# A hybrid transformer layer: attention values for four heads in one pass, the compressed branch laid among two delta-rule projections, and five staging tiles

## The chip, the core and the metric

The kernel runs on one core of a Trainium2 chip. A core has TensorE (PE in the rows; its weight loads are PEld), VectorE (DVE), ScalarE (ACT), GpSimd (POOL), and the queue of SyncE (SP), from which all transfers between HBM and the core's memory (SBUF) are issued here, in order. Matmul results land in banks of PSUM, from which VectorE and ScalarE copy them out. The metric is the time of one execution in microseconds; lower is better.

## The reference, cut to what matters

One layer works on 1024 tokens of width 1024, in fp32. Its input projection feeds three attention branches of 8 heads in 2 groups, and a gated delta rule of 4 heads; a feed-forward part follows.

```python
h = rmsnorm(x, norm1_g)
proj = h @ w_in
nsa_q, nsa_kv, nsa_gate, gdn_qkv, gdn_z, gdn_b, gdn_a = jnp.split(proj, SPLIT_POINTS, axis=-1)
...
o_cmp, p_cmp = nsa_compressed(q, k_cmp, kv[:, :, 1], cmp_pos, cmp_w1, cmp_w2)
idx = nsa_select_indices(p_cmp, T)
o_slc = nsa_selected(q, k_slc, kv[:, :, 3], idx)
o_win = nsa_window(q, k_win, kv[:, :, 5])
o_nsa = gates[..., 0:1] * o_cmp + gates[..., 1:2] * o_slc + gates[..., 2:3] * o_win
o_gdn = gdn_mixer(gdn_qkv, gdn_z, gdn_b, gdn_a, gdn_conv_w, gdn_a_log, gdn_dt_bias, gdn_norm_g)
x = x + jnp.concatenate([o_nsa, o_gdn], axis=-1) @ w_out
h = rmsnorm(x, norm2_g)
x = x + (jax.nn.silu(h @ w_gate) * (h @ w_up)) @ w_down
```

The compressed branch gathers overlapping blocks of 32 tokens' keys and values, adds a learned position to each token, sends each block through a small two-layer network (`cmp_w1`, a tanh form of the activation, `cmp_w2`), and attends to the 63 resulting vectors.

## The kernel before

A product of full precision is made of three matmuls: each operand is split into a rounded high half and a low half (ScalarE copies the high half, VectorE or GpSimd subtracts to get the low one), and `split3` (lines 119 to 121) issues high x high, high x low and low x high. The order of the work on each engine is not written by hand: an instruction scheduler places the rows, and the tile pools (tag and number of buffers) limit it.

*Start, 0 to 90 us.* x is staged in `xraw` tiles (3 buffers), split into `xh` and `xl`, and `proj_tok(c)` multiplies it, eight units of 128 tokens each, by pieces 0, 1 and 2 of the token-major weights. `wprep` loads weights in pieces through `wraw` (DMA L203), splits them on ScalarE (L205) and GpSimd (L208). `evac_z` stores what pieces 0 and 1 give, through `zt` tiles, to `zD`. Between them, x by tokens (`xN`) is loaded into the same `xraw` tiles and squared on ScalarE (L266), which gives `rstd1`, and the angles of the rotary embedding are worked out on VectorE and ScalarE (up to the sine, L307). Piece 2 is the compressed branch's keys and values; `evac_cmp` scales a unit into a `ck` tile (L331) and rotates it on GpSimd (L317 to L322).

*Compressed branch, 90 to 108 us.* `cmp_blocks` transposes the eight `ck` tiles (L340) into banks `b`; copies on VectorE (L345) and ScalarE (L346) lay them out by block into `kdt`; VectorE adds the positions (L360); 2 x 32 fp32 matmuls with `w1t` follow (L365), then tanh (L369), `hy` (L370) and the products with `w2t` (L375, L384), which end in `kch`, `kcl` and `vcs`. Zero tiles `zz` are stored to `uD` and `tD` (L398). Then the PSUM pool `psa` is closed and `pps` opened.

*Delta rule, 108 to 466 us.* `gdn_proj(ft)` (48 matmuls of 512 columns, a convolution, a store to `gD`) for ft = 0, 4, 1, 5, 2, 6, 3, 7, then the rest of the delta rule.

*Attention, 466 to 785 us.* 16 units (128 tokens, one group of 4 heads). `prep_q` loads `qt`, `scores` makes the window probabilities `Pw`, the selected ones `Ps` (two heads to a tile) and the compressed ones `PC`, `values` multiplies them with values. `merge` interleaves the scores of the next unit, the values of this one and a filler (`wob`: the delta rule's half of the output projection) by the costs that each yields or declares (`wa`, `wc`). `values(u)` goes over the unit's blocks once for each pair of heads `hp`: two blocks' transposes (4 of 128x128) fill a bank `b`, ScalarE (L1067) and VectorE (L1068) split it into `PT`, and, three `PT` tiles later, products of 256 columns (L1045) add into one bank `c`. After each pass ScalarE copies half of `c` to `otmp` (L1049) and VectorE adds the other half into `mn` (L1050).

*Feed-forward, from 785 us.* Not touched.

## Time and profile before

| | |
|---|---|
| median of 3 runs | 1499.25 us (1497.87 to 1504.8) |
| profiled execution | 1494.86 us, span 1493.1 us |
| TensorE | busy 1426.7 us, 96% of the span |
| its weight loads | 1220.1 us, 82% |
| VectorE | 966.9 us, 65% |
| ScalarE | 723.5 us, 48% |
| GpSimd | 708.1 us, 47% |
| mean granted clock | 0.985 of full speed |

The span runs from the first to the last instruction of the profiled execution. Matmuls overlap each other in the rows, so a duration of a matmul is longer than the distance to the next start; where matmuls follow each other, starts are compared. Shares are means over stages with different limits.

### The profile page before, as it was taken

Reading aid. Unit: us, or ns where it says so; the run is one execution under the profiler, and the core shown is the slowest. Engines: PE = TensorE matmul, PEld = TensorE weight load, DVE = VectorE, ACT = ScalarE, POOL = GpSimd, SP = SyncE. Lnnn points to the kernel's source line nnn. Section 1 sums busy time; section 2 is a strip of 40 time slices with the busy share of each in tenths; the row PEclk is TensorE's granted clock in tenths of the full one; section 3 lists DMA queues with packets and bytes.
Section 4 is the critical chain, followed back from the end, with each engine's and each line's share of the span. In section 5 each row is a group of like instructions: output and inputs, shape, how many; then the busy total and the mean of one; then the engine's idle time right before and its main releaser. Section 6 shows DMA issues by size and latency. Waiting matters only on the chain.

```text
span 1493.1 us, 23452 instructions
## 1 busy us (share of the span) xinstructions
PE 1426.7 (96%) x7984; PEld 1220.1 (82%) x7984; DVE 966.9 (65%) x2286; ACT 723.5 (48%) x1604; POOL 708.1 (47%) x755
## 2 busy tenths in 40 slices
...
GB/s 250 300 68 78 92 171 162 126 194 208 203 119 202 101 54 107 47 22 44 36 123 244 36 87 99 83 78 85 78 86 85 85 92 274 200 119 134 1 0 113
DMA packets 142743, 174.96 MB, mean 117 GB/s; under 512 B 26912, under 2 KB 79392, under 8 KB 142496
## 3 DMA queue, kind: packets, MB, share of 16 engines
...
q8 instruction: 63, 1.03, 0.3%
q14 instruction: 56, 0.46, 0.1%
...
## 4 chain that ended last, share of the span: by engine, by line
PE 60%; DVE 10%; issue 5%; ACT 5%; POOL 4%; DMA 2%; SPq 0%; POOLq 0%; ACTq 0%; DVEq 0%
PE mm L119 16%; PE mm L121 16%; PE mm L120 16%; PE c L1045 3%; PE b L1065 2%; DVE PT L1068 2%; ACT Ps L1016 1%; PE a L637 1%; DVE cy L429 1%; PE a L999 1%; PE a L644 1%; ACT PT L1067 1%; DMA wraw<-in_w_out 1%; POOL w L208 1%; DMA mgt<-mgD 1%
## 5 line engine op out<-in xcount | busy, mean ns | idle before, releaser
L1202 POOL TENSOR_TENSOR A<-wq,A 128x512 fp32r<-128x512 f32 x94 | 126.4, 1346 | 97.8 <-ACT A L1201 76.5
L1201 ACT ACTIVATE A<-wq 128x512 fp32r<-128x512 f32 x96 | 60.1, 630 | 135.0 <-PE mm L121 118.3
L119 PE MATMUL mm<-w,xh 128*128 128x256 f32 x384 | 112.2, 292 | 6.3 <-ACT w L205 3.9
L1068 DVE TENSOR_TENSOR PT<-b,PT 128x512 fp32r<-128x512 f32 (+2 forms) x168 | 103.8, 621 | 18.8 <-ACT PT L1067 17.0
L120 PE MATMUL mm<-w,xh 128*128 128x256 f32 x384 | 112.0, 292 | 1.0 <-POOL w L208 1.0
L121 PE MATMUL mm<-w,xl 128*128 128x256 f32 x384 | 111.9, 291 | 0.0
L1202 POOL TENSOR_TENSOR wk<-wq,wk 128x512 fp32r<-128x512 f32 x61 | 82.6, 1355 | 53.0 <-ACT wk L1201 44.7
L1067 ACT ACTIVATE PT<-b 128x512 fp32r<-128x512 f32 (+2 forms) x168 | 89.0, 538 | 37.4 <-PE b L1065 33.2
L1045 PE MATMUL c<-PT,vs 128*128 128x256 f32 x528 | 92.9, 300 | 0.1
L208 POOL TENSOR_TENSOR w<-wraw,w 128x512 fp32r<-128x512 f32 x48 | 63.5, 1337 | 60.6 <-ACT w L205 34.6
L1201 ACT ACTIVATE wk<-wq 128x512 fp32r<-128x512 f32 x63 | 39.6, 630 | 85.4 <-PE mm L121 78.5
L119 PEld LDWEIGHTS mm<-w,xh 128*128 128x128 f32 x384 | 75.3, 196 | 6.9 <-ACT w L205 4.1
L119 PE MATMUL mm<-T,A 128*128 128x512 f32 x200 | 79.2, 396 | 0.0
L120 PE MATMUL mm<-T,A 128*128 128x512 f32 x200 | 79.2, 396 | 0.0
L121 PE MATMUL mm<-T,A 128*128 128x512 f32 x200 | 79.2, 396 | 0.0
L1479 POOL TENSOR_TENSOR ring<-ring,ring 128x512 f32<-128x512 f32 x44 | 58.2, 1324 | 40.1 <-DVE ring L1464 26.5
L120 PEld LDWEIGHTS mm<-w,xh 128*128 128x128 f32 x384 | 75.5, 196 | 1.3 <-POOL w L208 1.2
L119 PE MATMUL mm<-xh,w 128*128 128x512 f32 x192 | 75.7, 394 | 0.0
L121 PEld LDWEIGHTS mm<-w,xl 128*128 128x128 f32 x384 | 75.4, 196 | 0.1
L121 PE MATMUL mm<-xh,w 128*128 128x512 f32 x192 | 75.3, 392 | 0.0
L1045 PEld LDWEIGHTS c<-PT,vs 128*128 128x128 f32 x528 | 73.0, 192 | 2.5 <-DVE PT L1068 0.3
L120 PE MATMUL mm<-xl,w 128*128 128x512 f32 x192 | 74.9, 390 | 0.0
...
## 6 DMA issues: line engine op xcount, KB each, us to landing
...
```

The lines of the kernel that those rows point to most:

```text
L119: after(mm(ps, lhsT=lh, rhs=rh, start=first, stop=False, skip_group_check=grow), prev)
L120: mm(ps, lhsT=lh, rhs=rl, start=False, stop=False, skip_group_check=grow)
L121: return mm(ps, lhsT=ll, rhs=rh, start=False, stop=last, skip_group_check=grow)
L208: (lo or G).tensor_tensor(out=wt[:, 1, k0:k0 + n, :], in0=raw, in1=f32(wt[:, 0, k0:k0 + n, :]), op=ALU.subtract)
L429: V.scalar_tensor_tensor(out=y, in0=cr[:, j:j + 512], scalar=cw[:, j:j + 1], in1=y, op0=ALU.mult, op1=ALU.add)
L1045: mm(po[:, 0:256], lhsT=v, rhs=PT[0:K, a, b_ * 256:(b_ + 1) * 256], start=(n_ == 0 and a == 0), stop=(last and b_ == len(vs) - 1 and a == 1))
L1065: tpose(pt[:, o_:o_ + P], src[:, hh, b * P:(b + 1) * P], ident)
L1067: act(out=PT[0:K, 0, 0:w], in_=pt[0:K, 0:w], func=AF.Copy)
L1068: V.tensor_tensor(out=PT[0:K, 1, 0:w], in0=pt[0:K, 0:w], in1=f32(PT[0:K, 0, 0:w]), op=ALU.subtract)
L1201: act(out=dst[:, 0], in_=src, func=AF.Copy)
L1202: after(eng.tensor_tensor(out=dst[:, 1], in0=src, in1=f32(dst[:, 0]), op=ALU.subtract), prev)
L1479: G.tensor_tensor(out=t, in0=half[o], in1=t, op=ALU.mult)
```

## The change

1. *Staging.* `xraw` has 5 buffers; the raw pieces of the first weights have a tag of their own, `w0raw`; the first x tile is loaded in two halves with the weights between; `wprep` stages through 4 raw tiles (the output projections keep 3). Small tiles (`lowr`, `sm`, `cs16`, `sn16`, `kch`, `kcl`) lie in another pool.
2. *Compressed branch.* `cmp_blocks(i - 1)` is called from `evac_cmp(i)`; the position adds come in pieces of 128x256 for each half of the tokens, those of jj = 0 on VectorE, those of jj = 1 on GpSimd. `w1t`, `w2t` and `cpt` are loaded ahead of `proj_tok(2)`. `gdn_proj` takes the bank function as an argument; `gdn_proj(0)` stands ahead of the 64 matmuls with `w1t`, `gdn_proj(4)` between them and the tanh.
3. *Values.* One pass over the blocks for all four heads: four transposes (one block, four heads), one split, two products of 512 columns; `otmp` and `mn` once for each unit. `Ps` has 4 buffers, `qt` 1; `wx` of the filler comes from the pool `pmx`, whose 3 buffers it shares with the mean's squares.

```diff
-    def wprep(src, K, w, lo=None, tag="w", bufs=2, pl=None, rawbufs=3, rawpl=None, hi=None):
+    def wprep(src, K, w, lo=None, tag="w", bufs=2, pl=None, rawbufs=4, rawpl=None, hi=None):
...
+    XB = 5
     for k in range(KD):
-        r = mk(p1, [P, T], "xraw", F32, 3)
-        dma(r, xT[:, k, :])
-        raw = mk(pw, [P, TOKW[0]], "wraw", F32, 3)
-        dma(raw, tok_src(0)[:, k, :])
+        r = mk(p1, [P, T], "xraw", F32, XB)
+        raw = mk(p1, [P, TOKW[0]], "w0raw", F32, XB)
+        for hf in range(2 if k == 0 else 1):
+            xs = slice(hf * 512, (hf + 1) * 512) if k == 0 else slice(0, T)
+            dma(r[:, xs], xT[:, k, xs])
+            if hf == 0:
+                dma(raw, tok_src(0)[:, k, :])
...
-        r = mk(p1, [P, D], "xraw", F32, 3)
+        r = mk(p1, [P, D], "xraw", F32, XB)
         dma(r, xN[i * P:(i + 1) * P, :])
...
+        if i > 0:
+            cmp_blocks(i - 1)
...
+                for jj in range(2):
+                    pos_j = cpt[:, a, 8 * jj:8 * jj + 8].unsqueeze(2)
+                    for g in range(2):
+                        (V if jj == 0 else G).tensor_tensor(out=kdt[a][jj][:, :, g, n0:n0 + 32],
+                                                            in0=kdt[a][1][:, :, g, n0:n0 + 32],
+                                                            in1=bc(pos_j, [P, 8, 32]), op=ALU.add)
...
-    proj_tok(2, evac_cmp, banka)
-    for i in range(NT):
-        cmp_blocks(i)
     w1t = mk(p1, [P, 2, 16, P], "w1t")
     dma(w1t, cw1)
...
+    proj_tok(2, evac_cmp, banka)
+    cmp_blocks(NT - 1)
+    gdn_proj(0, banka)
...
     for a in range(2):
...
-        for j in range(2):
-            pos_j = cpt[:, a, 8 * j:8 * j + 8].unsqueeze(2)
-            V.tensor_tensor(out=kdt[a][j].rearrange("p r g n -> p r (g n)"),
-                            in0=kdt[a][1].rearrange("p r g n -> p r (g n)"), in1=bc(pos_j, [P, 8, P]), op=ALU.add)
-        psh = banka("mm")
+        psh = pshs[a] = banka("mm")
...
+    gdn_proj(4, banka)
+    for a in range(2):
+        psh = pshs[a]
...
     for h in range(4):
-        gdn_proj(h)
-        gdn_proj(4 + h)
+        if h:
+            gdn_proj(h, bank)
+            gdn_proj(4 + h, bank)
...
-        qt = mk(pk, [P, 256], "qt", F32, 2)
+        qt = mk(pk, [P, 256], "qt", F32, 1)
...
-                Ps[hp] = mk(pn, [P, 2, T], "Ps", F32, 3)
+                Ps[hp] = mk(pn, [P, 2, T], "Ps", F32, 4)
...
+        Pw, Ps = u["Pw"], u["Ps"]
+        blocks = [None] + [(Pw, b, VS[:, i - np_ + b, 2 + g, :]) for b in range(np_ + 1)]
+        blocks += [(Ps, b, VS[:, b, g, :]) for b in range(i + 1)]
+        po = bank("c")
+
+        def products(n_, K, v, PT):
+            for a in range(2):
+                mm(po, lhsT=v, rhs=PT[0:K, a], start=(n_ == 0 and a == 0), stop=(n_ == len(blocks) - 1 and a == 1))
...
+        for n_, blk in enumerate(blocks):
+            pt = bank("b")
+            for h in range(4):
...
+            PT = mk(pn, [P, 2, 512], "PT", F32R, LAG + 1)
+            act(out=PT[0:K, 0], in_=pt[0:K], func=AF.Copy)
+            V.tensor_tensor(out=PT[0:K, 1], in0=pt[0:K], in1=f32(PT[0:K, 0]), op=ALU.subtract)
+            todo.append((n_, K, v, PT))
+            if len(todo) > LAG:
+                products(*todo.pop(0))
+            yield 0.6
...
+        tmp = mk(pn, [64, 512], "otmp", F32, 1)
+        act(out=tmp, in_=po[64:128], func=AF.Copy)
         for hp in range(2):
...
+            V.tensor_tensor(out=mn[hp * 64:(hp + 1) * 64, g * 2:g * 2 + 2, i * P:(i + 1) * P],
+                            in0=po[0:64, hp * 256:(hp + 1) * 256].rearrange("p (h t) -> p h t", h=2),
+                            in1=tmp[:, hp * 256:(hp + 1) * 256].rearrange("p (h t) -> p h t", h=2), op=ALU.add)
...
-        wx = mk(pn, [P, 512], "wx", F32, WXB)
+        wx = flat(mk(pmx, [P, 4, P], "wx", F32, 3))
...
-        return [0.3 + 0.35 + n * 0.3] * 2
+        return [0.6 * (n + 1) + 0.9]
```

**First place: TensorE behind the last projection.** Before, the last transposes (L340, from `ck` tiles into banks `b`) stand directly ahead of the matmuls with `w1t` (L365), and the first delta projection (`w_1136`) behind all of them.

```order
L340 MATMUL b_1038<-cst_75,ck_977 128x128
L340 MATMUL b_1038<-cst_75,ck_1010 128x128
L365 MATMUL mm_1062<-kdt_101_733,w1t_1054 128x126 [waits DMAHW7_49,DVE_49]
L365 MATMUL mm_1062<-kdt_101_733,w1t_1054 128x126 x7
L365 MATMUL mm_1062<-kdt_102_734,w1t_1054 128x126 [waits DVE_49,Activation_49]
L365 MATMUL mm_1062<-kdt_102_734,w1t_1054 128x126 x7
L375 MATMUL mm_1085<-hy_1079,w2t_1056 128x126 [waits DMAHW4_49,DVE_49]
```

Now (lines 373 and 401 are those transposes and matmuls, `w_1077` the weights of `gdn_proj(0)`, `w_1194` those of `gdn_proj(4)`; the left-out rows between are more of the same projection):

```order
L373 MATMUL b_985<-cst_75,ck_1014 128x128 [waits Activation_49,Pool_49]
L373 MATMUL b_987<-cst_75,ck_1014 128x128
L119 MATMUL mm_1086<-xh_89,w_1077 128x512
L120 MATMUL mm_1086<-xl_90,w_1077 128x512
L373 MATMUL b_987<-cst_75,ck_1049 128x128 [waits Activation_49]
L121 MATMUL mm_1086<-xh_89,w_1077 128x512
L373 MATMUL b_985<-cst_75,ck_1049 128x128 [waits Pool_49]
...
L121 MATMUL mm_1123<-xh_89,w_1077 128x512
L401 MATMUL mm_1160<-kdt_101_734,w1t_738 128x126 [waits DMAHW4_49,DVE_49]
L401 MATMUL mm_1160<-kdt_101_734,w1t_738 128x126 x7
L401 MATMUL mm_1160<-kdt_102_735,w1t_738 128x126 [waits Pool_49]
L401 MATMUL mm_1160<-kdt_102_735,w1t_738 128x126 x7
```

All 48 matmuls of `gdn_proj(0)` now stand between the last transposes and the first matmul with `w1t`.

**Second place: SP's queue ahead of proj_tok(2).** Before, three of its four weight pieces (`wraw` from `in_w_tok`) are issued ahead of `w1t`, and the fourth behind the store of `zt_604`, the sixth tile of `proj_tok(1)`:

```order
L203 DMA wraw_738<-in_w_tok 128x512 [waits DMAHW2_49,Pool_49]
L253 DMA zD_58<-zt_520 128x256 [waits DMAHW3_49,Activation_49]
L203 DMA wraw_742<-in_w_tok 128x512 [waits DMAHW4_49,Pool_49]
L203 DMA wraw_746<-in_w_tok 128x512 [waits DMAHW5_49,Pool_49]
L253 DMA zD_58<-zt_548 128x256 [waits DMAHW6_49,Activation_49]
L352 DMA w1t_1054<-in_cw 128x4096 [waits DMAHW7_49,PE_49]
L253 DMA zD_58<-zt_576 128x256 [waits DMAHW0_49,Activation_49]
L253 DMA zD_58<-zt_604 128x256 [waits DMAHW1_49,Activation_49]
L203 DMA wraw_750<-in_w_tok 128x512 [waits DMAHW2_49,Pool_49]
```

Now (`zt_605` is that sixth tile):

```order
L388 DMA w1t_738<-in_cw 128x4096 [waits DMAHW4_49,PE_49]
L257 DMA zD_58<-zt_549 128x256 [waits DMAHW5_49,Activation_49]
L257 DMA zD_58<-zt_577 128x256 [waits DMAHW6_49,Activation_49]
L390 DMA w2t_740<-in_cw 128x192 [waits DMAHW7_49]
L257 DMA zD_58<-zt_605 128x256 [waits DMAHW0_49,Activation_49]
L392 DMA cpt_742<-in_cpos 128x32 [waits DMAHW1_49]
L203 DMA wraw_745<-in_w_tok 128x512 [waits DMAHW2_49,Pool_49]
L203 DMA wraw_749<-in_w_tok 128x512 [waits DMAHW3_49,Pool_49]
L257 DMA zD_58<-zt_633 128x256 [waits DMAHW4_49,Activation_49]
L203 DMA wraw_753<-in_w_tok 128x512 [waits DMAHW5_49,Pool_49]
L203 DMA wraw_757<-in_w_tok 128x512 [waits DMAHW6_49,Pool_49]
```

All four pieces moved behind `w1t` and the sixth tile's store, the last two behind the seventh's too.

**Third place: TensorE in a unit's values.** Before, at the change from one pass to the next, the new pass opens bank `c` again and waits for VectorE:

```order
L1065 MATMUL b_6368<-cst_75,Ps_6153 128x128 [waits DVE_49,PE_49]
L1065 MATMUL b_6368<-cst_75,Ps_6153 128x128 x3
L999 MATMUL a_6380<-kss_788_4406,QS_5976 128x512 [waits PE_49]
L1045 MATMUL c_6376<-PT_6302,vcs_91 128x256 [waits DVE_49]
L1045 MATMUL c_6376<-PT_6302,vcs_91 128x256
L999 MATMUL a_6380<-kss_789_4407,QS_5976 128x512
L1045 MATMUL c_6376<-PT_6317,vs_5143 128x256 x4
```

Now a unit opens `c` once, with products of 512 columns (transposes L1062, products L1051):

```order
L1062 MATMUL b_6419<-cst_75,Pw_6140 128x128 x2
L1062 MATMUL b_6419<-cst_75,Pw_6201 128x128 x2
L1051 MATMUL c_6358<-PT_6364,vcs_85 128x512 [waits Activation_49]
L1051 MATMUL c_6358<-PT_6364,vcs_85 128x512
L1062 MATMUL b_6429<-cst_75,Pw_6140 128x128 [waits DVE_49]
L1062 MATMUL b_6429<-cst_75,Pw_6140 128x128
L1062 MATMUL b_6429<-cst_75,Pw_6201 128x128 x2
L1051 MATMUL c_6358<-PT_6383,vs_5156 128x512 [waits Activation_49]
```

Each bank `b` takes one block of two `Pw` (or `Ps`) tiles, four heads, and two wide products follow it where two to four narrow ones stood.

## Rows read from the trace of the kernel before

**Rows 1.** The page: the span, TensorE's busy time, and from the table of costliest groups the two halves of the PT split, all forms together (line, engine, operation, out<-in shapes, count | busy us, mean ns | idle time before and its releaser).

```profile
span 1493.1 us, 23452 instructions
...
PE 1426.7 (96%) x7984; PEld 1220.1 (82%) x7984; DVE 966.9 (65%) x2286; ACT 723.5 (48%) x1604; POOL 708.1 (47%) x755
...
L1068 DVE TENSOR_TENSOR PT<-b,PT 128x512 fp32r<-128x512 f32 (+2 forms) x168 | 103.8, 621 | 18.8 <-ACT PT L1067 17.0
...
L1067 ACT ACTIVATE PT<-b 128x512 fp32r<-128x512 f32 (+2 forms) x168 | 89.0, 538 | 37.4 <-PE b L1065 33.2
```
**Rows 2.** Busy time by stretch of the span, in the projection and compressed stage (stretch, its length, busy us and instructions of PE, PEld, DVE, ACT, POOL, then the mean granted clock, the DMA share and GB/s).

```profile
57.60:70.00 12.40, 7.52 (x51) 7.12 (x51) 6.96 (x34) 5.03 (x12) 4.03 (x7) 0.84 0.85 319
...
90.40:96.00 5.60, 2.09 (x18) 1.64 (x16) 3.29 (x9) 4.11 (x11) 3.31 (x6) 1.00 0.24 59
96.00:102.00 6.00, 4.83 (x30) 4.83 (x31) 4.52 (x4) 1.55 (x2) 0.00 (x0) 0.72 0.10 35
```
**Rows 3.** The same for 50 us of the attention stage.

```profile
685.00:735.00 50.00, 48.60 (x324) 41.55 (x324) 45.91 (x168) 38.97 (x92) 22.40 (x26) 1.00 0.10 33
```
**Rows 4.** The chain that ended last, followed back inside 485 to 785 us: shares of that stretch by engine, tile and line.

```profile
by line: PE c L1045 12.9%; PE b L1065 9.2%; DVE PT L1068 9.0%; ACT Ps L1016 7.1%; PE a L999 5.4%; issue 4.9%; PE mm L119 4.2%; ACT PT L1067 4.1%; PE mm L121 3.8%; PE mm L120 3.4%; DMA mgt<-mgD 3.2%; DVE Pw L953 3.0%; DVE Ps L1009 2.8%; PE a
```
**Rows 5.** The timeline behind the last projection (start us, length us, engine, line, operation, out<-in, count, idle before and its releaser).

```profile
90.27 0.28 PE L121 MATMUL mm<-w,xl 128*128 128x256 f32 x1
...
90.39 1.03 PE L340 MATMUL b<-cst,ck 128*128 128x128 f32 x8
...
93.47 1.06 PE L340 MATMUL b<-cst,ck 128*128 128x128 f32 x8 [2.04 <-ACT kdt L346]
94.14 1.72 DVE L345 COPY kdt<-b 64x256 f32<-64x256 f32 x4 [0.83 <-PE b L340]
...
95.89 4.63 DVE L360 TENSOR_TENSOR kdt<-kdt,cpt 128x1024 f32<-128x1024 f32 x4
...
97.17 5.22 PE L365 MATMUL mm<-kdt,w1t 128*128 128x126 f32 x32 [2.64 <-DVE kdt L360]
...
103.40 3.74 PE L365 MATMUL mm<-kdt,w1t 128*128 128x126 f32 x32
...
107.83 0.44 PE L384 MATMUL mm<-w2t,hy 128*63 128x64 f32 x4 [0.69 <-DVE hy L370]
...
108.20 0.50 PE L119 MATMUL mm<-xh,w 128*128 128x512 f32 x1
```
**Rows 6.** TensorE's timeline in the attention stage, two places: products with the compressed values, and products of blocks followed by a filler's three 512-column matmuls.

```profile
704.16 0.50 PE L1045 MATMUL c<-PT,vcs 64*128 64x256 f32 x2
704.59 0.47 PE L943 MATMUL a<-ksw,QS 128*128 128x192 f32 x2
...
716.82 0.60 PE L1065 MATMUL b<-cst,Ps 128*128 128x128 f32 x4
717.17 0.72 PE L1045 MATMUL c<-PT,vs 128*128 128x256 f32 x4
717.73 0.39 PE L119 MATMUL mm<-mgt,wo 128*128 128x512 f32 x1
717.96 0.39 PE L120 MATMUL mm<-mgt,wo 128*128 128x512 f32 x1
718.18 0.39 PE L121 MATMUL mm<-mgt,wo 128*128 128x512 f32 x1
```
**Rows 7.** Groups of instructions from 485 to 785 us, shapes kept apart (columns as in the table of rows 1).

```profile
L1068 DVE TENSOR_TENSOR PT<-b,PT 128x512 fp32r<-128x512 f32 x124 | 84.8, 686 | 11.7 <-ACT PT L1067 10.3
L1067 ACT ACTIVATE PT<-b 128x512 fp32r<-128x512 f32 x124 | 72.7, 591 | 33.1 <-PE b L1065 30.2 <-DVE sc L978 1.4 <-DVE PT L1068 0.3
...
L1045 PE MATMUL c<-PT,vcs 64*128 64x256 f32 x58 | 15.6, 337 | 5.6 <-DVE mn L1050 4.4 <-ACT PT L1067 0.9
...
L1049 ACT ACTIVATE otmp<-c 64x256 f32<-64x256 f32 x30 | 11.4, 382 | 5.3 <-PE c L1045 4.6
...
L872 POOL TENSOR_TENSOR qh<-qt,qh 128x256 fp32r<-128x256 f32 x10 | 7.4, 735 | 8.0 <-ACT qh L871 8.0
```
**Rows 8.** The timeline around the weights of proj_tok(2): the first and the last square over xN on ScalarE, a tile's evacuation, SP's issue of the fourth weight piece, its ScalarE copy, TensorE's wait, GpSimd's low half, and the first finished tile.

```profile
37.16 1.06 ACT L266 ACTIVATE xraw<-xraw 128x1024 f32<-128x1024 f32 x1 [3.71 <-DMA xraw<-in_xN]
...
51.30 1.06 ACT L266 ACTIVATE xraw<-xraw 128x1024 f32<-128x1024 f32 x1 [1.84 <-DMA xraw<-in_xN]
...
61.08 0.64 ACT L252 ACTIVATE zt<-mm 128x256 f32<-128x256 f32 x2
...
61.90 0.37 SPq L203 DMA_DIRECT2D wraw<-in_w_tok  x1
...
64.99 0.63 ACT L205 ACTIVATE w<-wraw 128x512 fp32r<-128x512 f32 x1 [3.27 <-DMA wraw<-in_w_tok]
...
65.67 0.38 PE L119 MATMUL mm<-w,xh 128*128 128x256 f32 x1 [3.92 <-ACT w L205]
65.69 1.27 POOL L208 TENSOR_TENSOR w<-wraw,w 128x512 fp32r<-128x512 f32 x1 [6.15 <-ACT w L205]
...
68.55 0.47 ACT L331 ACTIVATE ck<-mm,rstd 128x256 f32<-128x256 f32 x1 [1.69 <-PE mm L121]
```
**Rows 9.** Waits from 485 to 785 us, by engine and line (total us, times, longest us).

```profile
PE mm L119 <- DMA mgt<-mgD: 2.0, 1, 2.0
...
ACT PT L1067 <- PE b L1065: 31.5, 41, 2.4
```

More of the change, by code (lines that the diff above doesn't have):

```diff
@@ L174, in hybrid_block @@
     ident = C("ident")
-    lowr = mk(pcr, [P, P], "lowr", F32R)
     identr = mk(pcr, [P, P], "identr", F32R)
@@ L327, in hybrid_block, with gdn_proj @@
     cks = {}
+    def gdn_proj(ft, bank):
+        wt = wprep(w_gdn[:, ft], KD, P, tag="w")
+        prev = None
+        for hf in range(2):
+            hs = slice(hf * 512, (hf + 1) * 512)
+            ps = bank("mm")
+            for k in range(KD):
+                split3(ps, (wt[:, 0, k, :], wt[:, 1, k, :]), (xh[:, k, hs], xl[:, k, hs]), k == 0, k == KD - 1)
+            cr = mk(pw, [P, 515], "cr", F32, 2)
+            if hf == 0:
+                G.memset(cr[:, 0:3], 0.0)
+            else:
+                G.tensor_copy(cr[:, 0:3], prev[:, 512:515])
+            prev = cr
+            V.tensor_tensor(out=cr[:, 3:515], in0=ps, in1=rstdB[:, hs], op=ALU.mult)
+            cw = VC("conv")[:, ft * 4:ft * 4 + 4]
+            y = mk(pw, [P, 512], "cy", F32, 2)
+            act(out=y, in_=cr[:, 3:515], func=AF.Copy, scale=cw[:, 3:4])
+            for j in (2, 1, 0):
+                V.scalar_tensor_tensor(out=y, in0=cr[:, j:j + 512], scalar=cw[:, j:j + 1], in1=y,
+                                       op0=ALU.mult, op1=ALU.add)
+            th = mk(pw, [P, 512], "cth", F32, 1)
+            act(out=th, in_=y, func=AF.Tanh, scale=0.5)
+            V.scalar_tensor_tensor(out=y, in0=th, scalar=1.0, in1=y, op0=ALU.add, op1=ALU.mult)
+            dma(gD[ft, :, hs], y)
     def evac_cmp(i, ps):
@@ L556, in hybrid_block @@
             gram(c)
-        gdn_proj(8 + h)
+        gdn_proj(8 + h, bank)
     V.tensor_scalar(ssq, ssq, 4.0 * EPS, None, op0=ALU.add)
@@ L1026, in hybrid_block @@
     LAG = 3
-    WXB = 2
     def values(u):
@@ L1074, in values @@
-        for fn, a_ in todo:
-            fn(*a_)
-            yield 0.3
+        Pw, Ps = u["Pw"], u["Ps"]
[8 more added lines that the diff above has]
+            for h in range(4):
+                if blk is None:
+                    K, v = 64, vcs[:, g, :]
+                    tpose(pt[0:64, h * P:(h + 1) * P], PC[:, h, 1:65], ident)
+                else:
+                    src, b, v = blk
+                    K = P
+                    tpose(pt[:, h * P:(h + 1) * P], src[h // 2][:, h % 2, b * P:(b + 1) * P], ident)
+            PT = mk(pn, [P, 2, 512], "PT", F32R, LAG + 1)
[5 more added lines that the diff above has]
+            yield 0.6
```

80 lines of the change are left out of this document (11 added, 69 removed).

## The prediction

> **What bounds the kernel now.** I read the page first. TensorE is busy for 96% of the span [rows 1], so a gain must be TensorE time: columns, waits, or half clock. Then I tabulated the two stretches that the change rewrites. In the first, TensorE is busy for only 7.52 of 12.40 us from 57.6 to 70 us, for 2.09 of 5.60 from 90.4 to 96, and for 4.83 of 6.00 from there to 102; the granted clock falls to a mean of 0.84 and 0.72 of full speed on the way [rows 2]. That is a chain of dependent steps with nothing beside it. In the second, the attention stage of 485 to 785 us, three engines are close to full together: from 685 to 735 us TensorE shows 48.60, VectorE 45.91 and ScalarE 38.97 of 50 us [rows 3]. The chain that ends last runs there through several owners: value products 12.9%, transposes into `b` 9.2%, the two halves of the PT split on VectorE 9.0% and ScalarE 4.1%, softmax 7.1% [rows 4]. A TensorE saving there is paid out only in part.
>
> **Compressed branch.** The transposes behind the last projection begin at 90.39 and the first delta matmul at 108.20: 17.81 us. In it TensorE does 16 transposes, 64 w1 matmuls and six small products. The second 32 w1 matmuls take 3.74 us, hence up to 0.117 each; the first 32 take 5.22, after the clock had dropped. The rest is waits: 2.04 for ScalarE's copy, 2.64 for four VectorE adds of together 4.63 us, and 0.69 in front of each group of small products [rows 5]. The change puts 14 of the 16 transposes between projection units, the other two among the first delta matmuls, and 48 matmuls of 512 columns ahead of the w1 products. Three consecutive matmuls of 512 columns start 0.23 and 0.22 us apart [rows 6]; 48 of them give 48 x 0.225 = 10.8 us of cover. Behind it lie the last copies and the adds that belong to them, each now 128x256, a quarter of a former one, half of them on GpSimd. VectorE needs about 1.7 us of copies and 4 x 4.63/16 = 1.2 of adds [rows 5]. No row shows GpSimd's add of this shape; I take its 128x256 subtraction, 735 ns [rows 7], and get 4 x 0.74 = 3.0 us, behind a rope of four short operations and two weight splits of 1.27 [rows 8]: 5.5 us and the rope, within 10.8. gdn_proj(4), 10.8 us more, lets tanh and the w2 products run late, but at the pool change the next bank waits for `kcl` and `vcs`, the end of a chain of a tanh, a product, a copy and a subtraction; the present stop of 0.69 in front of a product is half of such a chain, so I put it at 1.4. On the path stay 16 x 0.0875 = 1.4 us of transposes (four take 0.35 from 716.82 to 717.17 [rows 6]), 64 x 0.117 = 7.5, small products 2 x 0.37 (107.83 to 108.20 [rows 5]) and 1.4: 11.0, so **7 us** are saved. Bounds: 5, if the w1 matmuls run 2 us late, and 8.2, if the pool change costs nothing.
>
> **Weights of proj_tok(2).** This is where the change can lose. Before, three of the four weight pieces were issued early; SP's queue issued the fourth at 61.90, behind the store of a tile that ScalarE evacuated at 61.08. Its ScalarE copy started at 64.99, and TensorE waited 3.92 us for that copy [rows 8]. After, all four stand behind the 2 MB `w1t` and that same store, two of them behind one more (the second difference shown with the change). GpSimd makes the low half of a piece in 1.27 us [rows 8], so three more pieces cost up to 3 x 1.27 = 3.8 us if the store leaves when it did. Against it, the store follows a ScalarE chain that starts from the last of eight squares over xN; two more staging tiles let their loads be issued up to two squares sooner. The squares start 14.14/7 = 2.0 us apart (37.16 to 51.30 [rows 8]), so the last can come 0 to 4 us earlier; I take the middle, 2, since the loads still have to share the DMA engines. The first projected tile, copied at 68.55 before [rows 8], then comes near 70.4. Net **+2 us** (3.8 - 2 = 1.8), bounds 0 and +5 (3.8 and a longer half clock). A first matmul that starts sooner only lengthens this wait, since the weights end it. The Trainium skill's page "TensorE: Matmul & The Clock Gate", section "What's actually happening", says that half clock is the default and that activity releases it; by that a longer pause costs twice, in waiting and in slow matmuls. The trace agrees: around the pause that ends at 65.67 the clock averages 0.84 [rows 2].
>
> **Values.** Each of the 16 units went over its blocks twice, with 256-column products, and now goes once with 512. With 128 contraction rows 528 products become 264. A 256-column matmul is followed 0.12 us later (90.27 to 90.39 [rows 5]), so a block's four take 0.48; four in a row from 717.17 to 717.73 take 0.56 with the drain of the transposes in it; two of 512 columns take 0.46 [rows 6]. Over 132 blocks that is 132 x 0.02 = 2.6 us, or 13 by the second spacing; I take 2.6, since the drain stays. Of the compressed values' products, with 64 rows, 64 become 32; a pair takes 0.43 us (704.16 to 704.59 [rows 6]) where other pairs take 0.24, so each carries 0.2 us beyond its columns; 16 pairs fewer give 3.2, or 6.4 if the extra goes with columns. Changing the pass makes TensorE wait for the single bank `c` behind VectorE's `mn`, 4.4 of 5.6 us [rows 7]; half of the hand-overs go, and the rest now lie behind four blocks' transposes. TensorE gives 2.6 + 3.2 + 4.4 = 10.2, up to 2.6 + 6.4 + 5.6 = 14.6. ScalarE had 89.0 us of splits [rows 1], and 148 of 512 columns at 591 ns are 87.5; its 32 `otmp` copies of 382 ns become 16 of about 591 [rows 7]: in all 1.5 + 2.8 = 4.3 us less. VectorE's 103.8 us of subtractions [rows 1] become 148 x 0.686 = 101.5 [rows 7]: 2.3 less. ScalarE waits 31.5 us for transposes [rows 9], so a faster TensorE feeds it at once; VectorE, 92% busy [rows 3], pays only its own 2.3. Between 2.3 and 14.6 I take **7.5 us**; bounds 1 and 15.
>
> The Trainium skill speaks otherwise of these sizes: the same page, section "Back-to-back issue gap", gives about 131 ns per 512-column matmul in a sustained stream. Estimated by it, a pair would fall by some 0.2 us and the products by over 25 us. The trace shows 0.22 to 0.23 us in a row [rows 6], so this gets no chance here.
>
> **At nothing.** `qt` gets one buffer, `wx` shares three with the mean's squares, `Ps` has four because one unit now holds two to its end, and small tiles change place. What covers them is that each is asked for a unit ahead, and a unit lasts some 19 us (300 us for 16); without that cover the price is the slow rival's.
>
> **The sum.** -7 + 2 - 7.5 = -12.5. The profiled execution took 1494.86 us (span 1493.1 [rows 1], and 1.8 around it), 4.4 under the median of 1499.25. On itself the sum gives 1482.4; on the median, against which a new median is compared, 1486.75: **1487**.
>
> **Rivals.**
> - *VectorE binds the values.* Its 45.91 of 50 us [rows 3] speaks for it, TensorE's share of the chain [rows 4] against it. Values give 1, the whole -7 + 2 - 1 = -6: 1493.
> - *TensorE binds them alone.* ScalarE's wait for transposes [rows 9] speaks for it. Values give 15, the whole -7 + 2 - 15 = -20: 1479.
> - *Late weights.* If the squares end no earlier, all four pieces follow the tile of 61.08: -7 + 5 - 7.5 = -9.5, 1490. For it speaks the queue's order alone, against it the loads that no longer wait.
> - *Slower: SP's queue stops behind `qt`.* A load of `qt` must now wait until GpSimd's subtraction (735 ns, which itself idles 8.0 us behind ScalarE [rows 7]) has read the former one. SP issues in order, so the filler's loads of `mgt`, `wo` and x2 stand behind it, and TensorE has already waited once for `mgt`, 2.0 us [rows 9]. Each unit that loses 12.5/16 = 0.78 us more than now eats the gain; at 1.8 us per unit, 29 us in all, the time is 1516. Against it: the load is asked for a unit ahead.
>
> **Chances.** Forecast 0.45 (own range 1480 to 1491), TensorE alone 0.17, VectorE binds 0.2, late weights 0.1, slower 0.08. A measurement can tell about 0.5%, 7.5 us, from no change: faster is below 1491.75, slower above 1506.75. Faster takes nearly all of the forecast, the 0.17, a quarter of the VectorE case and most of the late weights: 0.74; same 0.19; slower 0.07. The range runs from branch 8.2, weights 0 and values 15 (1476) to branch 5, weights +3.8 and values 1 (1497).
>
> **What would show it.** Right: w1 matmuls in one run without a wait above 0.5 us; 11 us instead of 17.8 of other than projection and delta work between the two; the first tile of proj_tok(2) copied between 68 and 71 us; no wait of value products for `mn`; the attention stage 7 us shorter with VectorE as busy as now. Wrong: a wait above 6 us for a split of proj_tok(2)'s weights; GpSimd adds far above 0.74 us; TensorE waiting for a DMA in every unit; an attention stage of unchanged length.

## The result and the profile after

The changed kernel took 1481.76 us (median of 4 runs, 1479.02 to 1482.18) against 1498.83 before: a ratio of 0.9885 with a 95% interval of 0.9857 to 0.9913. Two later measurements on other occasions gave 0.9905 (0.9886 to 0.9924) and 0.9897 (0.9866 to 0.9928). The profiled execution took 1479.02 us. So the gain is 14 to 17 us; the forecast said 1487 with a range of 1476 to 1497, that is 12.5 us under the median.

The page of the changed kernel, the rows that answer to [rows 1]:

```profile
span 1477.3 us, 22838 instructions
...
PE 1417.4 (96%) x7688; PEld 1194.4 (81%) x7688; DVE 965.9 (65%) x2270; ACT 717.6 (49%) x1568; POOL 715.0 (48%) x763
...
L1065 DVE TENSOR_TENSOR PT<-b,PT 128x512 fp32r<-128x512 f32 (+1 forms) x148 | 100.9, 685 | 17.4 <-ACT PT L1064 16.6
...
L1064 ACT ACTIVATE PT<-b 128x512 fp32r<-128x512 f32 (+1 forms) x148 | 86.1, 589 | 29.4 <-PE b L1062 27.7
```
TensorE's busy time fell by 9.3 us and the span by 15.8, so more than a third of the gain is time in which TensorE no longer stood still. The subtraction fell from 103.8 to 100.9 us, the ScalarE half from 89.0 to 86.1.

To see where the time went, four starts were read from each trace: the copy of the first tile of proj_tok(2) on ScalarE, the first gate matmul of the delta rule (L484 before, L497 after), the first transposes of `qh` (attention begins) and the weight load for the last attention normalisation; the fourth stretch ends at the first matmul of the final norm. In us:

| profile | first tile of proj_tok(2) | front: to the first gate matmul | delta rule | attention | feed-forward |
|---|---|---|---|---|---|
| before | 68.5 | 195.4 | 249.1 | 344.2 | 679.3 |
| after | 67.6 | 186.1 | 248.3 | 338.8 | 679.3 |
| after, second and third profile | 66.7, 67.5 | 185.3, 186.0 | 249.9, 249.8 | 337.0, 337.3 | 682.4, 682.5 |
| e1 values alone | 67.1 | 196.2 | 251.6 | 337.8 | 683.1 |
| e2 front alone | 67.5 | 186.1 | 249.1 | 344.5 | 683.7 |
| e3 compressed branch alone | 69.4 | 187.8 | 248.3 | 344.5 | 685.3 |
| e4 staging alone | 64.4 | 190.2 | 249.2 | 344.5 | 685.1 |
| e6 early weights | 69.2 | 189.0 | 249.8 | 337.0 | 680.3 |
| e9, e11 early weights, VectorE's split | 64.7, 65.2 | 183.2, 183.3 | 256.6, 249.3 | 337.6, 338.5 | 680.3, 680.3 |
| e10 two buffers of qt | 69.0 | 187.4 | 248.0 | 340.8 | 681.3 |
| e7 half the products | 68.0 | 186.5 | 248.1 | 317.0 | 679.1 |
| e8 no subtraction | 68.1 | 186.6 | 248.9 | 329.1 | 685.5 |

In the changed kernel's three profiles the front is shorter by 9.3 to 10.1 us than before's, and the attention by 5.4 to 7.2. Four more kernels have the same front (e2, e7, e8, e10: 186.1 to 187.4), and e1 has the old one (196.2). The feed-forward part, which no kernel touches, lies anywhere from 679.1 to 685.5: that is the execution, and it is why stages are compared here and not single totals. It goes with TensorE's granted clock: in that part TensorE had 3.4 us at 1.2 GHz, half of full speed, in before's profile and the changed kernel's first (679.3 both), 10.2 us in its second and third (682.4, 682.5) and 17.1 us in e3, e4 and e8 (685.1 to 685.5).

The front after, by stretches (columns as in [rows 2]):

```profile
56.00:70.00 14.00, 11.34 (x87) 10.34 (x86) 2.88 (x19) 6.10 (x14) 8.36 (x10) 1.00 0.75 228
70.00:80.00 10.00, 10.00 (x86) 10.00 (x86) 0.23 (x1) 1.76 (x4) 2.61 (x12) 1.00 1.03 402
80.00:89.10 9.10, 8.99 (x76) 8.79 (x75) 2.62 (x8) 2.56 (x7) 6.30 (x16) 1.00 0.06 20
89.10:104.00 14.90, 14.44 (x79) 12.03 (x78) 9.62 (x15) 7.44 (x13) 8.26 (x14) 1.00 0.17 53
104.00:118.00 14.00, 14.00 (x84) 12.33 (x83) 6.57 (x10) 1.94 (x5) 1.37 (x2) 1.00 0.18 57
```
Before, 57.6 to 70 us held 7.52 us of TensorE work in 12.40 at a mean clock of 0.84 [rows 2]; now 11.34 of 14.00, at full clock. TensorE's waits from 55 to 125 us, which are all that is listed there:

```profile
PE mm L120 <- POOL w L208: 2.5, 4, 1.0
PE mm L119 <- DVE kcl L417: 0.7, 1, 0.7
PE b L373 <- POOL ck L326: 0.5, 1, 0.5
PE mm L119 <- ACT w L205: 0.2, 1, 0.2
```
The 3.92 us in one piece [rows 8], with 1.0 behind it for a low half, became 2.5 us in four pieces of at most 1.0 and one of 0.2, and the waits of the compressed branch (2.04 and 2.64 [rows 5]) are gone. The branch itself, on the timeline after:

```profile
89.04 0.38 PE L373 MATMUL b<-cst,ck 128*128 128x128 f32 x2
...
92.36 3.00 DVE L383 TENSOR_TENSOR kdt<-kdt,cpt 128x256 f32<-128x256 f32 x4
...
93.66 2.75 POOL L383 TENSOR_TENSOR kdt<-kdt,cpt 128x256 f32<-128x256 f32 x4 [0.42 <-DVE kdt L383]
...
101.19 7.30 PE L401 MATMUL mm<-kdt,w1t 128*128 128x126 f32 x64
...
120.67 0.50 PE L119 MATMUL mm<-xh,w 128*128 128x512 f32 x1 [0.66 <-DVE kcl L417]
```
The last GpSimd adds end at 93.66 + 2.75 = 96.41, 4.8 us before the w1 matmuls need them; four take 2.75 us, 0.69 each, and VectorE's four beside them 3.00. The 64 w1 matmuls run in one go, 7.30 us or 0.114 each. The end of the chain (`kcl`) makes the first matmul in the new pool wait 0.66 us.

### The profile page after: what moved, and what is told of

Its sections match the earlier page's. It is cut to its first block, busy times and chain, and to the rows that moved or that the text cites. A ratio compares the mean times of both kernels' runs of the same rounds, so it can differ in the third digit from the quotient of the medians.

```text
span 1477.3 us, 22838 instructions
## 1 busy us (share of the span) xinstructions
PE 1417.4 (96%) x7688; PEld 1194.4 (81%) x7688; DVE 965.9 (65%) x2270; ACT 717.6 (49%) x1568; POOL 715.0 (48%) x763
## 4 chain that ended last, share of the span: by engine, by line
PE 61%; DVE 9%; issue 5%; POOL 5%; ACT 4%; DMA 3%; SPq 0%; POOLq 0%; DVEq 0%; ACTq 0%
PE mm L121 16%; PE mm L119 16%; PE mm L120 16%; PE c L1051 3%; PE b L1062 2%; DVE PT L1065 2%; PE a L1012 2%; PE a L650 1%; DVE cy L353 1%; ACT Ps L1029 1%; ACT PT L1064 1%; PE a L657 1%; POOL sqa L1640 1%; DMA mgt<-mgD 1%; PE a L964 1%
## 5 line engine op out<-in xcount | busy, mean ns | idle before, releaser
L119 PE MATMUL mm<-w,xh 128*128 128x256 f32 x384 | 110.6, 288 | 2.5 <-ACT kst L593 2.3
L120 PE MATMUL mm<-w,xh 128*128 128x256 f32 x384 | 110.0, 286 | 2.5 <-POOL w L208 2.5
L1065 DVE TENSOR_TENSOR PT<-b,PT 128x512 fp32r<-128x512 f32 (+1 forms) x148 | 100.9, 685 | 17.4 <-ACT PT L1064 16.6
L1064 ACT ACTIVATE PT<-b 128x512 fp32r<-128x512 f32 (+1 forms) x148 | 86.1, 589 | 29.4 <-PE b L1062 27.7
L1051 PE MATMUL c<-PT,vs 128*128 128x512 f32 x264 | 90.8, 430 | 0.1
L120 PEld LDWEIGHTS mm<-w,xh 128*128 128x128 f32 x384 | 73.5, 191 | 3.4 <-POOL w L208 3.3
L119 PEld LDWEIGHTS mm<-w,xh 128*128 128x128 f32 x384 | 73.5, 191 | 3.1 <-ACT kst L593 2.5
L1513 DVE TENSOR_TENSOR B<-B,mm 128x512 f32<-128x512 f32 x100 | 63.6, 678 | 16.1 <-PE mm L121 15.6
```

The lines of the kernel that those rows point to most:

```text
L119: after(mm(ps, lhsT=lh, rhs=rh, start=first, stop=False, skip_group_check=grow), prev)
L120: mm(ps, lhsT=lh, rhs=rl, start=False, stop=False, skip_group_check=grow)
L1051: mm(po, lhsT=v, rhs=PT[0:K, a], start=(n_ == 0 and a == 0), stop=(n_ == len(blocks) - 1 and a == 1))
L1064: act(out=PT[0:K, 0], in_=pt[0:K], func=AF.Copy)
L1065: V.tensor_tensor(out=PT[0:K, 1], in0=pt[0:K], in1=f32(PT[0:K, 0]), op=ALU.subtract)
L1513: V.tensor_tensor(out=out_, in0=a_, in1=b_, op=op)
```

## The experiments

**Which part gives what.** Four kernels with one part or two of the change; the hunks are those of the diff above, taken whole.

e1 (part 3, and the small tiles' place):

```diff
-                Ps[hp] = mk(pn, [P, 2, T], "Ps", F32, 3)
+                Ps[hp] = mk(pn, [P, 2, T], "Ps", F32, 4)
...
+        po = bank("c")
+
+        def products(n_, K, v, PT):
```

> The kernel before with the third part alone (values in one pass, buffers of qt, Ps and wx, and the small tiles' place). By the two traces the attention stage gave 5.4 us: 1493.5, ratio 0.9964. If the forecast's 7.5 us were right and only the trace of the changed kernel were unlucky: 1491.5. If VectorE binds the stage, the wait of value products for mn (4.4 us in seven waits before) is gone, but waits of score matmuls for VectorE's maxima of 5 us or more stand in its place.

Measured: 1494.39 us, ratio 0.9950 (0.9928 to 0.9972); attention 337.8 us, 6.4 less than before. The mn wait is down to 0.2 us, and score matmuls wait in its place, as the reading that VectorE binds had it: 5.7 us for VectorE's maximum at L943 and 3.6 at L999:

```profile
PE a L943 <- DVE mx L957: 5.7, 8, 1.3
PE a L999 <- DVE mx L1009: 3.6, 4, 2.2
```
e2 (parts 1 and 2):

```diff
+    XB = 5
...
+    gdn_proj(0, banka)
```

> The kernel before with the first and second part (staging and compressed branch), values as before. By the two traces these parts gave 9.3 to 10 us up to the delta rule: 1489, ratio 0.9936. If the parts were not independent (a shift of the later stages against their transfers), it would differ by more than 2 us from the whole change's gain less that of the values alone.

Measured: 1492.45 us, ratio 0.9947 (0.9922 to 0.9973); front 186.1, as in the whole change. The total lies 3.4 us above the 1489 expected while the front is as expected; the feed-forward part had 683.7. The two halves add up: 9.3 in the front, 6.4 in the values, against 15.5 in the whole (788.7 to 773.2 us at the last attention normalisation).

e3 (part 2 alone):

```diff
-    proj_tok(2, evac_cmp, banka)
-    for i in range(NT):
-        cmp_blocks(i)
...
+    proj_tok(2, evac_cmp, banka)
+    cmp_blocks(NT - 1)
+    gdn_proj(0, banka)
```

> The kernel before with the compressed branch alone, staging through 3 tiles as before. The branch itself hides 8 us. If the earlier xN squares of five staging tiles are needed for the weights of proj_tok(2) to come in time, as the forecast supposed, this loses 2 to 4 us of it again: 1493 to 1495 and the first tile of proj_tok(2) copied after 69.5 us. If the order of the queue helps by itself (GpSimd's weight splits no longer run beside VectorE's angle chain), the first tile comes near 69 or before and the time is near 1490.

Measured: 1489.52 us, ratio 0.9942 (0.9916 to 0.9967); front 187.8, first tile 69.4. The tile lies at the border between the two readings, the time and the front (7.6 us less than before) with the second: the new order of the queue costs little even with three staging tiles, 0.9 us at the first tile against before's profile and 2.3 against e1's.

e4 (part 1 alone):

```diff
-    def wprep(src, K, w, lo=None, tag="w", bufs=2, pl=None, rawbufs=3, rawpl=None, hi=None):
+    def wprep(src, K, w, lo=None, tag="w", bufs=2, pl=None, rawbufs=4, rawpl=None, hi=None):
...
-        r = mk(p1, [P, T], "xraw", F32, 3)
+        r = mk(p1, [P, T], "xraw", F32, XB)
```

> The kernel before with five staging tiles and four raw tiles alone; the compressed branch as before. Forecast's reading: the squares end about 3.5 us earlier, and proj_tok(2)'s four weight pieces can all be issued early, so TensorE's wait of 3.9 us for the fourth goes: 1495 to 1496. If GpSimd's splits beside VectorE's angle operations set the end, those operations still take 1.2 us instead of 0.22 and half of that is lost: 1497 to 1498.

Measured: 1495.16 us, ratio 0.9965 (0.9946 to 0.9984); first tile 64.4, front 190.2. Part 1 alone is worth 5.2 us in the front: with four raw tiles all of proj_tok(2)'s weights are issued by 50.5 us, and TensorE does not stop:

```profile
56.00:70.00 14.00, 14.00 (x121) 14.00 (x120) 7.14 (x36) 4.33 (x10) 3.77 (x10) 1.00 0.80 304
...
47.70 1.34 SPq L203 DMA_DIRECT2D wraw<-in_w_tok  x3
...
50.16 0.38 SPq L203 DMA_DIRECT2D wraw<-in_w_tok  x1
```
VectorE's long operations beside GpSimd's splits, the second reading of the expectation, are there (`sm` takes 1.54 us), but they do not hold the first tile up. Together the two parts give 9.3 to 10.1 and not 12.8: the new order of SP's queue, with `w1t` ahead of the weights, takes some 3 us of part 1's gain back.

**The changed kernel again**, for the variation between profiles (no edit).

> The changed kernel unaltered, beside the three others of this call, so that stages are compared on one chip. The traces so far show the untouched feed-forward part with 679 us in some profiles and 685 in others; if that is the execution and not the kernel, it varies here too, and the sum of values alone (-6.5 us up to 788 us) and front alone (-9.0) should stand in this one's first 785 us: about -15.5 there.

Measured: 1482.06 us, ratio 0.9905; 16.5 us less at the last attention normalisation, and a feed-forward part of 682.4 instead of 679.3.

**Can those 3 us be had?** e6:

```diff
+    wt2 = wprep(tok_src(2), KD, TOKW[2])
     w1t = mk(p1, [P, 2, 16, P], "w1t")
     dma(w1t, cw1)
...
-    proj_tok(2, evac_cmp, banka)
+    proj_tok(2, evac_cmp, banka, wt2)
```

> The changed kernel with one thing moved: proj_tok(2)'s weights are prepared ahead of the load of w1t, as before, all four pieces through the four raw tiles. If the late weights are what the compressed branch's new order costs (staging alone brought the first tile of proj_tok(2) to 64.4 us, with the new order it comes at 67.6), the first tile comes near 64.5 and everything after it 3 us sooner: ratio 0.002 below the changed kernel's. If GpSimd's splits slow VectorE's angle chain again (operations of 1.2 us instead of 0.22) and that chain sets the end, the first tile stays at 67 or later and nothing is gained.

Measured: 1486.11 us, ratio 0.9940 (0.9919 to 0.9960); first tile 69.2, front 189.0, 3 us worse than the changed kernel. But neither theory's reason holds. Rows of e6's timeline, ScalarE:

```profile
65.70 0.63 ACT L205 ACTIVATE w<-wraw 128x512 fp32r<-128x512 f32 x1 [2.21 <-DMA wraw<-in_w_gdn]
68.67 0.63 ACT L205 ACTIVATE w<-wraw 128x512 fp32r<-128x512 f32 x1 [2.34 <-DMA wraw<-in_w_gdn]
69.20 0.82 ACT L362 ACTIVATE ck<-mm,rstd 128x256 f32<-128x256 f32 x2
```
TensorE's rows around the same time, the last product of the second tile and the next thing it does (in brackets its idle time before, and what ended it), and GpSimd's, a low half of gdn_proj(0)'s weights and the first row of the first tile's rotation:

```profile
66.11 0.28 PE L121 MATMUL mm<-w,xl 128*128 128x256 f32 x1
71.59 0.69 PE L373 MATMUL b<-cst,ck 128*128 128x128 f32 x2 [5.20 <-POOL ck L326]
...
69.38 1.26 POOL L208 TENSOR_TENSOR w<-wraw,w 128x512 fp32r<-128x512 f32 x1 [1.70 <-ACT w L205]
70.60 0.25 POOL L321 TENSOR_TENSOR rp<-ck,cs 128x32 f32<-128x32 f32 x1
```
The first two tiles, 24 products each, were multiplied by 66.4, the first of them by about 63.5. TensorE then stood still for 5.20 us, because the first tile's copy (69.20) stood in ScalarE's queue behind the two copies of gdn_proj(0)'s weights, the second of which waited until 68.67 for its transfer, and the tile's rotation (70.60) stood in GpSimd's queue behind the low half of the same weights. So e9 splits those weights on VectorE, both halves, which takes them out of both queues at once:

```diff
-        wt = wprep(w_gdn[:, ft], KD, P, tag="w")
+        wt = wprep(w_gdn[:, ft], KD, P, tag="w", hi=V if ft == 0 else None, lo=V if ft == 0 else None)
```

> The early weights of proj_tok(2) once more, with one more edit: the weights of gdn_proj(0) are split by VectorE alone (high and low half), so that they no longer stand in ScalarE's and GpSimd's queues ahead of the first tile of proj_tok(2). With the weights early, ScalarE copied that tile only at 69.20 us, behind a copy of those weights that waited for its transfer until 68.67. If that queue was what ate the gain, TensorE works from 60.6 us on without a stop, the first tile comes at 64.5, proj_tok(2) ends near 85.5 instead of 89.0, and the time is 3 to 4 us below the changed kernel's. If GpSimd's splits beside VectorE's angle chain are the reason, VectorE's operations of 1.2 to 1.5 us show again and the tile comes no earlier than 67.

> The kernel with early weights of proj_tok(2) and VectorE's split for gdn_proj(0), again, now beside the changed kernel on one chip. In its first profile TensorE did not stop from 56 to 70 us and the delta rule's gate matmuls came 2 to 3 us sooner than in the changed kernel's profiles (183.2 against 186.1 and 185.3), but the execution lost 7 us later, in the scan. If that loss was the execution's own, this profile has the same first 200 us and none of the loss, and the median lies 2 to 4 us under the changed kernel's. If it comes from the edit (other transfers that meet the scan's), it shows again between 313 and 440 us.

Measured: e9 1477.70 us, ratio 0.9878 (0.9846 to 0.9911), e11 1480.60, ratio 0.9886 (0.9848 to 0.9924). The first tile comes at 64.7 and 65.2, the front is 183.2 and 183.3, 2.0 to 2.9 us shorter than in the changed kernel's three profiles. The queues were what ate it; which of the two ate more, no run tells. VectorE's long operations are there in e9 as well (`sm` takes 1.51 us), so they were not the reason. The 7 us lost in e9's delta rule (256.6) did not come again in e11 (249.3) and belong to that execution. The clock accounts for them: e9, from 310 to 335 us (columns as in [rows 2]):

```profile
310.00:335.00 25.00, 23.43 (x154) 22.39 (x154) 2.85 (x7) 11.13 (x32) 8.13 (x16) 0.73 0.75 207
```
25 us at a mean of 0.73 lose 25 x 0.27 = 6.8 us of full-speed work; e11 has 3.4 us at 1.2 GHz in its whole delta rule, e9 has 20.5. In total time, beside e9 and e11 in the same measurements, two forms of the changed kernel took 1481.24 (e10) and 1484.11 (e12): 3.5 us more both times, which is the sign and size of the front's gain, but the intervals of the ratios overlap, so the totals alone don't show it.

> The changed kernel unaltered, for comparison with the run beside it: 1481 to 1483, and again 185 to 186 us at the delta rule's gate matmuls.

Measured: 1484.11 us, ratio 0.9897; front 186.0.

**The slow rival undone.** e10:

```diff
-        qt = mk(pk, [P, 256], "qt", F32, 1)
+        qt = mk(pk, [P, 256], "qt", F32, 2)
```

> The changed kernel with two buffers of qt again (the slow rival undone). If the single buffer holds up SP's queue in the units, the attention stage gets shorter, by up to 16 times what a unit loses; if the load is asked for early enough, as forecast, it stays within 1 us of 337 to 339 us (from the first qh transpose to the last use before the feed-forward part), and the time is the changed kernel's.

Measured: 1481.24 us, ratio 0.9893 (0.9862 to 0.9925); attention 340.8 us, 0.8 us beyond the expected stretch on the long side. Its clock was lower: 17.1 us of the stage at 1.2 GHz, against 6.8 to 13.7 in the changed kernel's three profiles. A second buffer makes nothing shorter, so no cost of the single one is seen.

**Who binds the attention stage.** e7 and e8:

```diff
-            for a in range(2):
-                mm(po, lhsT=v, rhs=PT[0:K, a], start=(n_ == 0 and a == 0), stop=(n_ == len(blocks) - 1 and a == 1))
+            mm(po, lhsT=v, rhs=PT[0:K, 0], start=(n_ == 0), stop=(n_ == len(blocks) - 1))
```

> The changed kernel without the second product of each block (the low half is still split off, but not multiplied; the output lacks it). TensorE loses 148 matmuls of 512 columns, 148 x 0.23 to 0.25 = 34 to 37 us. If TensorE binds the attention stage, the stage (311 us from 434 to 770 less what is untouched) gets some 30 us shorter; if VectorE does, 10 us or less.

Measured: 1457.29 us; attention 317.0, 20 to 21.8 us less than the changed kernel's 337.0 to 338.8.

```diff
-                mm(po, lhsT=v, rhs=PT[0:K, a], start=(n_ == 0 and a == 0), stop=(n_ == len(blocks) - 1 and a == 1))
+                mm(po, lhsT=v, rhs=PT[0:K, 0], start=(n_ == 0 and a == 0), stop=(n_ == len(blocks) - 1 and a == 1))
...
-            V.tensor_tensor(out=PT[0:K, 1], in0=pt[0:K], in1=f32(PT[0:K, 0]), op=ALU.subtract)
```

> The changed kernel without VectorE's subtraction of PT; both products use the high half, so TensorE does as much as before (the output lacks the low half). VectorE loses 148 x 0.686 = 101 us. If VectorE binds, the stage falls until TensorE's own columns and the softmax bind, 20 us or more; if TensorE binds, 10 us or less.

Measured: 1474.85 us; attention 329.1, 7.9 to 9.7 us less. In e7 148 products of 512 columns go, 148 x 0.23 = 34 us (0.23 is the step between two 512-column matmuls in [rows 6], 717.73 to 717.96), and six tenths of them come off the stage, between the two readings of the expectation; in e8 VectorE's 148 subtractions go, which take 72.8 us off its busy time (965.9 to 893.1 on the pages), and about an eighth of them comes off. Both ran the units' first 20 us at a mean clock of 0.66, lower than the changed kernel's (below), so both shares may be a little low. TensorE binds the stage for the most part, VectorE by itself nearly not.

## Why the forecast held, and which terms were off

The range and the sign held, and the measured gain of 14 to 17 us is a little more than the 12.5 forecast. That the sum came so near is in part luck: one term had the wrong sign, and another the right size for reasons that were not in it. By the marks, the front was taken as -7 + 2 = -5 and is -9.3 to -10.1; the values as -7.5 and are -5.4 to -7.2. Point by point:

*Compressed branch, forecast -7.* The last projection matmul of proj_tok(2) is followed at 89.04 us by transposes (90.39 before), and the front ends at 186.1 (195.4 before): what lies between fell from 105.0 to 97.1, by 7.9 us. Of these, 12 x 0.0875 = 1.1 (the rate of [rows 6]) are transposes that now stand ahead of that mark, so the branch gave 6.8. The step is right in its terms on the path too: w1 matmuls without a wait at 0.114, and 0.66 instead of 1.4 at the pool change. Under the cover GpSimd's adds took 0.69 instead of 0.74, but VectorE's last four took 3.00 us instead of 1.2; the chain still ended 4.8 us before it was needed.

*Weights of proj_tok(2), forecast +2, bounds 0 and +5.* **This step failed**, on the side of a gain: the projection ended 1.35 us earlier with those 1.1 us of transposes inside, -2.4 in all. (e1, whose front is the old one, had its first tile at 67.1, 1.4 us before the profile of before: that much of it can be the execution.) The queue is as it was read. What went wrong is the price: the sum let the sixth tile's store leave 2 us earlier, because it took only the squares into account. The rows that answer to [rows 8], ScalarE's last square, the copies of tiles, GpSimd's low halves and the first tile of proj_tok(2):

```profile
47.78 1.06 ACT L270 ACTIVATE xraw<-xraw 128x1024 f32<-128x1024 f32 x1 [1.11 <-DMA xraw<-in_xN]
...
55.92 0.37 ACT L256 ACTIVATE zt<-mm 128x256 f32<-128x256 f32 x1
...
60.10 1.38 ACT L205 ACTIVATE w<-wraw 128x512 fp32r<-128x512 f32 x2 [3.40 <-DMA wraw<-in_w_tok]
...
67.57 0.48 ACT L362 ACTIVATE ck<-mm,rstd 128x256 f32<-128x256 f32 x1 [0.23 <-PE mm L121]
...
60.81 2.51 POOL L208 TENSOR_TENSOR w<-wraw,w 128x512 fp32r<-128x512 f32 x2 [9.07 <-ACT w L205]
64.05 5.02 POOL L208 TENSOR_TENSOR w<-wraw,w 128x512 fp32r<-128x512 f32 x4 [0.72 <-ACT w L205]
```
The last square starts at 47.78 instead of 51.30, 3.5 us earlier; the sixth tile is copied at 55.92 instead of 61.08, 5.2 us earlier. The rest, 1.7 us, was won between the two, where ScalarE no longer copies weights and VectorE's chain to the sine is shorter. This second part is the term that the sum put at nothing, and it is the steadier one: from the last square to the sixth tile it is 9.8 us before and in e1, 8.1, 7.3 and 7.3 in the changed kernel's profiles, and 6.8 in e3, which has the new order alone. The last square itself starts at 49.1 to 51.3 with three staging tiles (e3, e1, before) and at 47.8 to 50.5 with five, so the 2 us taken for it are not shown wrong. Rows of that chain before, VectorE's work on `sm` and two of the eight angle steps, and GpSimd's weight splits:

```profile
54.41 1.50 DVE L275 TENSOR_TENSOR sm<-sm,rstd 128x256 f32<-128x256 f32 x1 [1.66 <-POOL rstd L268]
...
57.17 1.23 DVE L305 SCALAR_TENSOR_TENSOR ang<-nn,ang 128x64 f32<-128x64 f32 x1
58.44 1.19 DVE L305 SCALAR_TENSOR_TENSOR ang<-nh,ang 128x64 f32<-128x64 f32 x1
...
54.35 1.29 POOL L208 TENSOR_TENSOR w<-wraw,w 128x512 fp32r<-128x512 f32 x1
57.03 2.51 POOL L208 TENSOR_TENSOR w<-wraw,w 128x512 fp32r<-128x512 f32 x2 [1.40 <-ACT w L205]
```
and after:

```profile
51.78 0.43 DVE L279 TENSOR_TENSOR sm<-sm,rstd 128x256 f32<-128x256 f32 x1 [1.57 <-POOL rstd L272]
...
53.62 0.22 DVE L309 SCALAR_TENSOR_TENSOR ang<-nn,ang 128x64 f32<-128x64 f32 x1
```
`sm` took 1.50 us before and 0.43 after, an angle step 1.23 and 1.19 against 0.22, and the long ones are those that run while GpSimd splits a weight piece (54.35 to 55.64, and 57.03 to 59.54 in two). Putting the weights late, which the forecast counted as a loss, took the splits out from beside this chain. In e4 and e6, where splits stand beside it again, the chain ends at 59.5 and 60.3 us, in the changed kernel's profiles at 54.8 to 55.8. The chain matters here only because the late weights' loads stand behind the sixth tile's store: in e4 and e9, whose weights are issued early, it ends at 59.5 and 61.0 us and the first tile still comes at 64.4 and 64.7. Against those two the late weights cost 2 to 3 us all the same.

The second half of the failed step: three more pieces at GpSimd's pace were to cost 3.8 us in a row. They do come 1.26 us apart, with one gap of 0.72, but TensorE works on each piece as it arrives, so the waits are 2.5 us in four pieces and the clock stays at full where it had fallen. e4 and e9, with no wait at all, have the first tile at 64.4 and 64.7.

*Values, forecast -7.5, bounds 1 and 15.* Right in size, but not by its terms. A block now shows on TensorE's timeline as

```profile
690.60 0.73 PE L1051 MATMUL c<-PT,vcs 64*128 64x512 f32 x2
691.26 0.49 PE L119 MATMUL mm<-mgt,wo 128*128 128x512 f32 x1
...
694.83 0.60 PE L1062 MATMUL b<-cst,Ps 128*128 128x128 f32 x4
695.19 0.71 PE L1051 MATMUL c<-PT,vs 128*128 128x512 f32 x2
695.73 0.60 PE L1062 MATMUL b<-cst,Ps 128*128 128x128 f32 x4
```
0.36 us of transposes and 0.54 of products, 0.90 in all, against 0.35 + 0.56 = 0.91 before [rows 6]: 132 x 0.01 = 1.3 us, where 2.6 was taken. Products of 64 rows: a pair of 512 columns takes 0.66 us (690.60 to 691.26) for two former pairs of 0.43, so 16 x (0.86 - 0.66) = 3.2 us, as taken. The 4.4 us for bank `c` are gone, but score matmuls wait instead for VectorE to free their banks, and e1 shows the same two waits, so they belong to the edit:

```profile
PE a L956 <- DVE mx L970: 5.8, 8, 1.3
PE a L1012 <- DVE mx L1022: 3.9, 4, 2.2
...
PE a L964 <- DVE mx L966: 1.6, 4, 0.6
```
Before, score matmuls waited for such maxima 1.5, 1.3 and 0.5 us, 3.3 in all, against 5.8 + 3.9 + 1.6 = 11.3 now. Other waits got shorter, so the stage as a whole, before and after, shows

```profile
444.50:788.70 344.20, 323.86 (x2106) 278.79 (x2106) 275.53 (x1103) 261.21 (x684) 180.88 (x223) 0.98 0.26 85
434.40:773.20 338.80, 317.63 (x1811) 258.18 (x1810) 276.68 (x1083) 254.91 (x649) 181.16 (x223) 0.98 0.26 87
```
TensorE stood still for 344.20 - 323.86 = 20.3 us before and for 338.80 - 317.63 = 21.2 after. The term of 4.4 for the waits should have been nothing, and the 5.4 us come from TensorE's own time, which fell by 6.2. Added up over the stage from each start to the next, without the idle time, the compressed values' products and transposes give 2.9 us of that (21.5 to 18.6), the other blocks' 2.4 (126.3 to 123.9) and the filler 1.1 (84.1 to 83.0); the score matmuls' 83.7 did not change.

Part of it is the clock, which the term left out. The second 20 us of the stage, where the units begin, before, after, and in the changed kernel's second profile:

```profile
464.50:484.50 20.00, 17.03 (x77) 14.22 (x77) 14.92 (x84) 15.26 (x61) 4.58 (x5) 0.66 0.73 262
...
454.40:474.40 20.00, 17.12 (x73) 13.42 (x74) 14.68 (x86) 15.63 (x60) 4.71 (x5) 0.74 0.74 268
...
455.20:475.20 20.00, 15.66 (x78) 11.99 (x79) 14.91 (x88) 16.52 (x62) 5.22 (x6) 0.91 0.81 285
```
The mean granted clock there is 0.61 to 0.66 in the four profiles with the old values (before, e2, e3, e4) and 0.74 to 0.91 in the eight with the new ones and nothing left out, so the difference goes with the edit. Twenty us times it is 1.6 to 5.0 us against before's profile, an estimate that counts the whole stretch as TensorE's. Why the clock stays up with the new values, no run shows.

*Rivals.* "VectorE binds the values" falls by e8, though score matmuls now wait 11.3 us for it; "late weights" by the first tile (67.6, earlier than the 68 to 71 that the forecast named for itself); "stops behind `qt`" by e10. "TensorE alone" overstated: 0.6 of its time is paid.
